# First layer: Q and K of head 0 for both halves of the tokens from a float32 product ahead of the norm

## The chip, the cores and the metric

The kernel runs on one core of a Trainium2 chip. What counts is the time of one execution on the device, in microseconds (us). All inputs and outputs are float32.

## The reference

A decoder of two layers works on 1024 tokens of width 1024. Each layer normalises h, makes one input projection from it, runs two groups of heads side by side and adds their output projection to h; then it adds a gated feed-forward part:

```
u = rmsnorm(h, attn_norm[l])
rq, rk, rv, rg, dq, dk, dv = split(u @ w_in[l])
ret = silu(rg) * rmsnorm(retention_chunkwise(rq, rk, rv))
dif = rmsnorm(diff_attention(dq, dk, dv, lam)) * (1 - lam_init)
h = h + concat(ret, dif) @ w_out[l]
u = rmsnorm(h, ffn_norm[l])
h = h + (silu(u @ w_gate[l]) * (u @ w_up[l])) @ w_down[l]
```

The change touches only the start of the first layer: its rmsnorm, and dq, dk, dv of head 0. Differential attention has four heads. Each head has two softmaxes of 64 channels and uses their difference; it is causal, with a bias that falls with distance. The norm's factor is one number per token, so it may be put on before a projection or after it. The norm's gains are one number per channel and may be folded into the weights.

## The kernel before

Everything is kept channels by tokens: h is eight tiles of 128 channels by 1024 tokens. The tokens are worked in two halves of 512. A product that must be nearly float32 is made in the faster float32r format: each operand is split into a high and a low part, and three matmuls of the parts (high by high, high by low, low by high) go into the same PSUM bank (`mm3`, L288 to L290, for a weight as the stationary operand; `tm_pair`, L323 to L325, for the values, where the tokens are stationary). A weight is split by a cast on ScalarE (L280) and a subtraction on GpSimd (L281); it stands in tiles named `w`, of which there are 12. The normalised tokens are split in `norm_half`: VectorE multiplies (L446), ScalarE casts (L448), VectorE or, for two of the eight tiles of half 0, GpSimd subtracts (L450).

The norm of a half comes in three steps. ScalarE squares and VectorE sums (L426, L433); TensorE adds over the channels with small matmuls (L398); a few tiny operations make the factor of each token, and TensorE spreads it over the partitions by transposing it (L414, into a bank of tag `s`). Then the 24 large operations of the split follow.

K and Q of head 0 for half 0 are special in the first layer. `fm_first` (L307) multiplies h itself, ahead of the norm, by weights into which the gains are folded (L1232), in full float32. When the factor is there, it is put on as the product leaves PSUM (L696), and `stack` writes the high part (L522, ScalarE) and the low part (L523, VectorE) of K and Q into stacked tiles. K and Q of half 1 are made after the norm, with `mm3`.

TensorE runs its instructions in the order in which the program writes them; on the other engines a scheduler chooses the order, and each engine then runs it strictly in a row, as does SyncE's queue of DMAs. The program's order around the change is: K of half 0, Q of half 0, with the norm's small matmuls in between; the values of half 0, with the transposes of half 1's norm (L414) between them; then head 0. Attention goes over eight blocks of 128 queries. `att_block` makes the scores of softmax 1 (L574, L575, into one of two banks of tag `s`), then of softmax 0, then transposes the weights of the block before (`att_turn`, L600). VectorE adds the bias and takes the maximum (L577, L580), ScalarE takes the exponential (L581), VectorE the reciprocal of the sum (L582) and the weighting (L656), ScalarE scales (L657), VectorE combines both (L666), and the transposes of this block need that. Every second block, `att_out` multiplies by the values (L619 to L622) and ScalarE copies the result (L624).

So that TensorE need not wait for that chain, `weave` puts matmuls of something else between the steps. It is given two totals: each unit of the attention draws total of fill by total of attention. The attention of blocks 0 to 3 has 72 units, its fill 96: 48 for K and Q of half 1 and 48 for the values of half 1. Blocks 4 to 7 are filled with K and Q of head 1. If the fill runs out early, the attention's steps stand alone.

Of the kernel before, what the change touches and what calls it, by code (L numbers as in the profile page):

```python
# [13 lines left out]
R32 = mybir.dt.float32r  # L14
AF = mybir.ActivationFunctionType
ALU = mybir.AluOpType
AX = mybir.AxisListType

P = 128
D = 1024  # L20
T = 1024
KT = D // P
NH = 2
HT = T // NH
# [95 lines left out]
class Line:  # L120
# [17 lines left out]
    def run(self, end):  # L138
        self.todo()
        while self.n + 1 < end:  # L140
            self.n += 1
            go, after = self.products[self.n]
            yield from go()
            self.todo()
            after()


class Trunk:
# [152 lines left out]

    def fm_first(self, h, ws):

        for w in ws:
            ps = self.bank("mm")
            for k in range(KT):
                self.nc.tensor.matmul(ps, lhsT=w[:, P * k:P * k + P], rhs=h[k][:, 0:HT], start=k == 0,  # L307
                                      stop=k == KT - 1)
                yield 4
            self.first_ps.append(ps)  # L310

    def tm_pair(self, w2, u, tt):
        ps = self.bank("mm")
# [122 lines left out]
    def norm_half(self, h, hf, gcol, us, lag=11, gap=9, first=False, keep=False):  # L436
        nc = self.nc
        sl = slice(hf * HT, hf * HT + HT)
        parts = self.squares(h, sl, 0, True, first)
        yield lag  # L440
        y = yield from self.rsqrt_rows(parts, D, gap=gap)
        hi = self.t("u", 4, [P, KT, HT], R32)
        lo = self.t("u", 4, [P, KT, HT], R32)
        for k in range(KT):
            f = self.tmp()
            nc.vector.scalar_tensor_tensor(out=f, in0=h[k][:, sl], scalar=self.gains[:, gcol + k:gcol + k + 1],  # L446
                                           in1=y, op0=ALU.mult, op1=ALU.mult)
            nc.scalar.copy(hi[:, k], f)  # L448
            eng = nc.gpsimd if keep and k in (1, 4) else nc.vector
            eng.tensor_tensor(out=lo[:, k], in0=f, in1=hi[:, k].bitcast(F32), op=ALU.subtract)  # L450
        if keep:
            self.first_y = self.big("sp")[:, 0:HT]
            nc.scalar.copy(self.first_y, y)
        us[hf] = (hi, lo)

    def seven_first(self, h, gcol, b, keep):
# [230 lines left out]
    def attention(self, l, us, w_first, norm1):  # L687
        wk, wq, wdv = w_first
        nc = self.nc
        v, qk, outs = {}, self.qk_tiles(), []  # L690
        kq = lambda hf: self.chain(self.stacks(wk, us, (hf,), qk[1], 1.0), self.stacks(wq, us, (hf,), qk[0], 0.125))
        first = [self.chain(kq(hf), self.values(wdv, us, hf, v)) for hf in range(NH)]
        if l == 0:
            for ps, st, scale in zip(self.first_ps, (qk[1], qk[0]), (1.0, 0.125)):
                f = self.tmp()
                nc.vector.tensor_tensor(out=f, in0=ps, in1=self.first_y, op=ALU.mult)  # L696
                self.stack(f, st, slice(0, HT), scale)
            self.weave(norm1, 40, self.values(wdv, us, 0, v), 48)
            self.late_consts()
        else:  # L700
            self.weave(norm1, 96, first[0], 96)
        self.prev, self.norms, self.outs = None, [], []
        for h in range(4):
            o = self.big("mx")
            outs.append(o)
            A = self.att_open(h, qk, v, o)
            nqk = self.qk_tiles() if h < 3 else None
            self.att_swap(A, 0)
            if h:
                self.att_swap(A, 1)  # L710
            if h == 0:
                self.weave(self.att_part(l, A, 0, 4), PART0, first[1], 96)
                self.att_swap(A, 1)
            elif h == 2:
                self.weave(self.att_part(l, A, 0, 4), PART0, self.values(wdv, us, 1, v), 48)
            if h == 3:
                rq = [self.big("ka") for _ in range(2)]
                rk = [self.big("a4") for _ in range(2)]
                fill = self.chain(self.ret_proj(us, rq[0], 1.0), self.ret_proj(us, rq[1], 1.0),
                                  self.ret_proj(us, rk[0], 0.125), self.ret_proj(us, rk[1], 0.125))  # L720
            else:
                fill = self.qk_head(us, nqk)
            if h % 2:
                self.weave(self.att_part(l, A, 0, 8), PART0 + PART1, fill, 96 if h == 1 else 192)
            else:
                self.weave(self.att_part(l, A, 4, 8), PART1, fill, 96)
            if h < 3:
                qk = nqk
            if h == 1:
                wdv = [self.weight(), self.weight()]  # L730
                v = {}
                self.weave(self.att_close(l), 48, self.values(wdv, us, 0, v), 48)
        return outs, rq, rk
# [481 lines left out]
    def run(self):  # L1215
        nc = self.nc
        self.nf = 0
        h = [self.big("a4") for _ in range(KT)]
        raws = [self.big("wr") for _ in range(2)]
        fold = [self.big("sp") for _ in range(2)]  # L1220

        def load(hf, ks):
            sl = slice(hf * HT, hf * HT + HT)
            for k in ks:
                nc.sync.dma_start(h[k][:, sl], self.a["xT"][k][:, sl])

        def load_w(i, c):
            cs = slice(512 * c, 512 * c + 512)
            nc.sync.dma_start(raws[i][:, cs], self.a["wts"][i][:, cs])
            g = self.gains[:, 4 * c:4 * c + 4].rearrange("p (k o) -> p k o", o=1).broadcast_to([P, 4, P])  # L1230
            v = lambda t: t[:, cs].rearrange("p (k m) -> p k m", m=P)
            nc.vector.tensor_tensor(out=v(fold[i]), in0=v(raws[i]), in1=g, op=ALU.mult)  # L1232

        def some(n):
            for _ in range(n):
                next(early)
        us, nus = {}, {}
        for c in range(2):
            load_w(0, c)
            load(0, range(4 * c, 4 * c + 4))  # L1240
        for c in range(2):
            load_w(1, c)
        self.wi = 2
        self.first_ps = []
        early = self.fm_first(h, fold)
        norm0 = self.norm_half(h, 0, 0, us, keep=True, gap=14)
        norm1 = self.norm_half(h, 1, 0, us, 8, 14, True)
        next(norm0)
        some(6)
        next(norm0)  # L1250
        load(1, range(KT))
        next(norm1)
        some(4)
        self.drain(norm0, early)
        wk, wq = [self.weight(raw=r) for r in raws]
        wdv = [self.weight(), self.weight("mx")]
        w_first = (wk, wq, wdv)
        h = self.layer(0, h, us, w_first, norm1, lambda h: [self.norm_half(h, 0, 8, nus)])
        h = self.layer(1, h, nus, self.first_weights(), self.norm_half(h, 1, 8, nus, 34),
                       lambda h: [self.final(h, 0, HT, 0), self.final(h, HT, 256, 0)])  # L1260
        self.drain(self.final(h, HT + 256, 256, 1))
# [28 lines left out]
```

## Time and profile before

| | us |
|---|---|
| median of three runs | 2290.36 (2289.78 to 2291.29) |
| the profiled execution's own time | 2289.39 |
| its span, first to last instruction | 2287.6 |
| TensorE busy | 2251.1 |
| VectorE busy | 1404.7 |
| ScalarE busy | 1009.1 |
| GpSimd busy | 731.7 |

In the profile PE is TensorE's matmuls, PEld its weight loads, DVE VectorE, ACT ScalarE, POOL GpSimd, SP SyncE. A row of the timeline gives the start, the duration, the engine, the source line, the operation, the tile written and the tiles read, and how many instructions are merged; behind it in brackets the idle time before it and who ended it. The end of a matmul is modelled, so the distance of two starts tells more of TensorE's pace than the duration of one. A float32 matmul of 128x512 shows as two records. In the table of windows the number behind the busy times is the clock that TensorE was granted, 1.00 being full. Names such as `ps_mm` are tiles: `ps_` means PSUM.

### The profile page before, as it was taken

How to read it: one execution, taken by the hardware profiler on the slowest of the kernel's cores; microseconds unless marked ns; L12 is line 12 of the kernel's file. 1: busy time of each engine (PE TensorE's matmuls, PEld its weight loads, DVE VectorE, ACT ScalarE, POOL GpSimd, SP SyncE). 2: the span in 40 equal slices, each digit the busy share in tenths (PEclk: the TensorE clock that was granted, in tenths of full speed). 3: DMA queues.
4: the chain of work that ended last, by engine and by line, in shares of the span. 5: the costliest groups of instructions: out<-in, count | busy, mean ns of one | idle time of the engine just before them, and what ended most of it. 6: DMA issues, size and time to landing. Idle time of an engine off the chain costs nothing.

```text
span 2287.6 us, 30632 instructions
## 1 busy us (share of the span) xinstructions
PE 2251.1 (98%) x11328; PEld 1895.3 (83%) x11328; DVE 1404.7 (61%) x2596; ACT 1009.1 (44%) x1905; POOL 731.7 (32%) x588
## 2 busy tenths in 40 slices
PE   7999999999999999999999999999999999999998
PEld 5888898787888888888888888988878888888887
DVE  8777612989534333995567774059884434359856
ACT  5666523445333333543256665234453333344332
POOL 3111212120455555335121112211215445544350
PEclk9999999999999999999999999999999999999999
DMA  4212121112433333652232222112123232346422
GB/s 164 79 47 65 44 95 38 55 57 63 137 106 103 105 106 90 230 186 96 72 99 56 56 65 88 52 37 74 49 95 120 93 115 93 110 148 202 157 65 74
DMA packets 74215, 216.58 MB, mean 95 GB/s; under 512 B 8017, under 2 KB 10065, under 8 KB 74065
## 3 DMA queue, kind: packets, MB, share of 16 engines
q1 hardware_dynamic: 74064, 214.62, 29.1%
q8 instruction: 89, 1.46, 0.3%
q14 instruction: 62, 0.50, 0.1%
HBM read 162.16 MB, written 44.04 MB: 90 GB/s over the span
## 4 chain that ended last, share of the span: by engine, by line
PE 84%; DVE 11%; ACT 2%; issue 1%; DMA 1%; POOL 0%; SPq 0%; DVEq 0%; ACTq 0%; POOLq 0%
PE ps_mm L264 8%; PE ps_mm L265 8%; PE ps_mm L266 8%; PE ps_mm L289 7%; PE ps_mm L288 7%; PE ps_mm L290 7%; PE ps_s L265 4%; PE ps_s L264 4%; PE ps_s L266 4%; PE ps_mm L323 3%; PE ps_mm L324 3%; PE ps_mm L325 3%; PE ps_t L265 2%; PE ps_t L264 2%; PE ps_t L266 2%
## 5 line engine op out<-in xcount | busy, mean ns | idle before, releaser
L241 POOL TENSOR_TENSOR w<-wr,w 128x512 fp32r<-128x512 f32 x262 | 368.2, 1419 | 442.9 <-ACT w L240 425.6
L281 POOL TENSOR_TENSOR w<-wr,w 128x512 fp32r<-128x512 f32 x140 | 186.2, 1337 | 577.3 <-ACT w L280 520.7
L288 PE MATMUL ps_mm<-u,w 128*128 128x512 f32 (+1 forms) x735 | 296.1, 403 | 0.0
L289 PE MATMUL ps_mm<-u,w 128*128 128x512 f32 (+1 forms) x735 | 287.2, 391 | 2.4 <-DVE u L450 2.4
L290 PE MATMUL ps_mm<-u,w 128*128 128x512 f32 (+1 forms) x735 | 286.5, 390 | 0.0
L240 ACT CAST w<-wr 128x512 fp32r<-128x512 f32 x312 | 187.2, 619 | 136.5 <-DVE wr L911 77.5
L264 PE MATMUL ps_mm<-u,w 128*128 128x512 f32 x432 | 168.5, 390 | 0.0
L266 PE MATMUL ps_mm<-u,w 128*128 128x512 f32 x432 | 168.1, 389 | 0.0
L265 PE MATMUL ps_mm<-u,w 128*128 128x512 f32 x432 | 168.1, 389 | 0.0
L290 PEld LDWEIGHTS ps_mm<-u,w 128*128 128x128 f32 x735 | 138.1, 188 | 30.1
L289 PEld LDWEIGHTS ps_mm<-u,w 128*128 128x128 f32 x735 | 138.6, 189 | 26.0 <-DVE u L450 3.1
L288 PEld LDWEIGHTS ps_mm<-u,w 128*128 128x128 f32 x735 | 138.3, 188 | 23.7
L960 ACT COPY t<-ps_mm 128x512 f32<-128x512 f32 x76 | 44.7, 588 | 240.3 <-PE ps_mm L266 240.3
L280 ACT CAST w<-wr 128x512 fp32r<-128x512 f32 x140 | 85.7, 619 | 128.6 <-PE ps_t L289 39.6
L325 PE MATMUL ps_mm<-w,u 128*128 128x256 f32 x448 | 127.2, 284 | 0.8 <-DVE u L450 0.8
L323 PE MATMUL ps_mm<-w,u 128*128 128x256 f32 x448 | 128.0, 286 | 0.0
L324 PE MATMUL ps_mm<-w,u 128*128 128x256 f32 x448 | 126.9, 283 | 0.0
L241 POOL TENSOR_TENSOR w<-t,w 128x512 fp32r<-128x512 f32 x48 | 65.1, 1357 | 191.9 <-ACT w L240 191.9
L577 DVE CUSTOM_DVE_ANT_0 sp<-ps_s,wr 128x512 f32<-128x512 f32 (+2 forms) x192 | 102.9, 552 | 32.3 <-PE ps_s L575 31.3
L581 ACT ACTIVATE sp<-sp,m 128x256 f32<-128x256 f32 (+7 forms) x128 | 99.2, 775 | 50.2 <-DVE m L580 49.4
L869 DVE TENSOR_TENSOR a<-a,ps_mm 128x512 f32<-128x512 f32 (+1 forms) x148 | 98.6, 667 | 27.6 <-PE ps_mm L266 14.5
L909 DVE TENSOR_TENSOR t<-wr,wr 128x512 f32<-128x512 f32 x46 | 32.8, 712 | 119.2 <-DMA wr<-wts 118.5
(386 smaller groups left out, 5919.7 us busy)
## 6 DMA issues: line engine op xcount, KB each, us to landing
wr<-wts SPq DMA_DIRECT2D x190, 512.0 KB, 3.7
mx<-s_fast SPq DMA_DIRECT2D x56, 512.0 KB, 4.9
s_fast<-mx SPq DMA_DIRECT2D x48, 512.0 KB, 4.8
kb<-ka SPq DMA_DIRECT2D x64, 128.0 KB, 2.3
s_rest<-mx SPq DMA_DIRECT2D x12, 512.0 KB, 2.9
kb<-wts SPq DMA_DIRECT2D x12, 512.0 KB, 5.4
mx<-s_rest SPq DMA_DIRECT2D x12, 512.0 KB, 3.3
a<-xT SPq DMA_DIRECT2D x16, 256.0 KB, 5.4
```

Of the source, the lines that this page charges most:

```text
L240: nc.scalar.copy(h, src)
L241: (eng or nc.gpsimd).tensor_tensor(out=o, in0=src, in1=h.bitcast(F32), op=ALU.subtract)
L264: mm(ps, lhsT=wh[:, c], rhs=bh, start=first and i == 0, stop=False, skip_group_check=True)
L265: mm(ps, lhsT=wh[:, c], rhs=bl, start=False, stop=False, skip_group_check=True)
L266: mm(ps, lhsT=wl[:, c], rhs=bh, start=False, stop=i == 3, skip_group_check=True)
L281: nc.gpsimd.tensor_tensor(out=o, in0=raw[:, cols], in1=h.bitcast(F32), op=ALU.subtract)
L288: mm(out, lhsT=lh, rhs=rh, start=first, stop=False)
L289: mm(out, lhsT=lh, rhs=rl, start=False, stop=False)
L290: mm(out, lhsT=ll, rhs=rh, start=False, stop=last)
L323: mm(o, lhsT=uh, rhs=wh, start=k == 0, stop=False)
L324: mm(o, lhsT=uh, rhs=wl, start=False, stop=False)
L325: mm(o, lhsT=ul, rhs=wh, start=False, stop=k == KT - 1)
```

## The change

`fm_first` now makes four products instead of two: K and Q of half 0 into two `mm` banks, K and Q of half 1 into the bank of tag `o` and one of tag `t`, each of eight float32 matmuls. `first_stacks` puts the factors on and writes the stacked tiles, for each half once its norm is done. The stacked tiles of head 0 come from other pools (`mx`, `ka`), since those of `h` are still read. The weights of K and Q are no longer split. Both halves' norms are now given by the same helper, the factor of half 1 is kept too, and the whole of it stands ahead of the values of half 0, which are no longer woven with the norm. Blocks 0 to 3 of head 0 still have a fill total of 96, but only the values of half 1 (48) are left in it.

```diff
     def fm_first(self, h, ws):
-        for w in ws:
-            ps = self.bank("mm")
+        for (hf, w), tag in zip([(hf, w) for hf in range(NH) for w in ws], ("mm", "mm", "o", "t")):
+            ps = self.bank(tag)
+            self.first_ps.append(ps)
             for k in range(KT):
-                self.nc.tensor.matmul(ps, lhsT=w[:, P * k:P * k + P], rhs=h[k][:, 0:HT], start=k == 0,
-                                      stop=k == KT - 1)
+                self.nc.tensor.matmul(ps, lhsT=w[:, P * k:P * k + P], rhs=h[k][:, HT * hf:HT * hf + HT],
+                                      start=k == 0, stop=k == KT - 1)
                 yield 4
-            self.first_ps.append(ps)
+
+    def first_stacks(self, qk, hf):
+        for ps, st, scale in zip(self.first_ps[2 * hf:], (qk[1], qk[0]), (1.0, 0.125)):
+            f = self.tmp()
+            self.nc.vector.tensor_tensor(out=f, in0=ps, in1=self.first_y[hf], op=ALU.mult)
+            self.stack(f, st, slice(HT * hf, HT * hf + HT), scale)
...
-            eng = nc.gpsimd if keep and k in (1, 4) else nc.vector
+            eng = nc.gpsimd if keep and hf == 0 and k in (1, 4) else nc.vector
...
-        first = [self.chain(kq(hf), self.values(wdv, us, hf, v)) for hf in range(NH)]
+        first = [self.chain(*([] if l == 0 else [kq(hf)]), self.values(wdv, us, hf, v)) for hf in range(NH)]
         if l == 0:
-            for ps, st, scale in zip(self.first_ps, (qk[1], qk[0]), (1.0, 0.125)):
-                f = self.tmp()
-                nc.vector.tensor_tensor(out=f, in0=ps, in1=self.first_y, op=ALU.mult)
-                self.stack(f, st, slice(0, HT), scale)
-            self.weave(norm1, 40, self.values(wdv, us, 0, v), 48)
+            self.drain(first[0])
...
-        norm0 = self.norm_half(h, 0, 0, us, keep=True, gap=14)
-        norm1 = self.norm_half(h, 1, 0, us, 8, 14, True)
+        self.first_y = []
+        self.first_qk = [self.big("mx", R32) for _ in range(2)], [self.big("ka", R32) for _ in range(2)]
+        norm0, norm1 = [self.norm_half(h, hf, 0, us, first=True, keep=True) for hf in range(NH)]
         next(norm0)
-        some(6)
+        some(8)
         next(norm0)
         load(1, range(KT))
         next(norm1)
-        some(4)
-        self.drain(norm0, early)
-        wk, wq = [self.weight(raw=r) for r in raws]
-        wdv = [self.weight(), self.weight("mx")]
-        w_first = (wk, wq, wdv)
-        h = self.layer(0, h, us, w_first, norm1, lambda h: [self.norm_half(h, 0, 8, nus)])
+        some(3)
+        self.drain(norm0)
+        some(5)
+        self.first_stacks(self.first_qk, 0)
+        some(8)
+        next(norm1)
+        some(3)
+        self.drain(norm1, early)
+        self.first_stacks(self.first_qk, 1)
+        w_first = (None, None, [self.weight(), self.weight()])
+        h = self.layer(0, h, us, w_first, None, lambda h: [self.norm_half(h, 0, 8, nus)])
```

The lines of the changed kernel differ: L308 is the float32 matmul (before L307), L404 and L420 the norm's small matmuls and transposes (L398, L414), L329 to L331 the values (L323 to L325), L452, L454 and L456 the split (L446, L448, L450), L315 the product with the factor (L696), L528 and L529 `stack` (L522, L523), L580 and L581 the scores (L574, L575), L606 the transposes (L600), L587 the exponential (L581), L663 the scaling (L657), L630 the copy of the output (L624); L280 and L288 to L290 keep theirs.

TensorE's queue at the end of the start-up, before the change (`ps_mm_193` is Q of half 0, `ps_s_294` the sums of half 1's norm, `ps_mm_308` the values of half 0):

```order
L307 MATMUL ps_mm_193<-a_19_94,sp_100 128x512
L307 MATMUL ps_mm_193<-a_20_95,sp_100 128x512
L307 MATMUL ps_mm_193<-a_21_96,sp_100 128x512
L398 MATMUL ps_s_294<-c_ones,acc_168 128x1 x4
L323 MATMUL ps_mm_308<-w_261,u_201 128x256
L324 MATMUL ps_mm_308<-w_262,u_201 128x256
L325 MATMUL ps_mm_308<-w_261,u_202 128x256
```

The same place now (`ps_o_259` and `ps_t_281` are K and Q of half 1, `ny_275` is the factor of half 1's norm):

```order
L308 MATMUL ps_o_259<-a_21_96,sp_99 128x512
L404 MATMUL ps_s_269<-c_ones,acc_174 128x1 x4
L308 MATMUL ps_t_281<-a_14_89,sp_100 128x512
L308 MATMUL ps_t_281<-a_15_90,sp_100 128x512
L308 MATMUL ps_t_281<-a_16_91,sp_100 128x512
L420 MATMUL ps_s_285<-c_ident,ny_275 128x128 x4
L308 MATMUL ps_t_281<-a_17_92,sp_100 128x512
L308 MATMUL ps_t_281<-a_18_93,sp_100 128x512
L308 MATMUL ps_t_281<-a_19_94,sp_100 128x512
L308 MATMUL ps_t_281<-a_20_95,sp_100 128x512
L308 MATMUL ps_t_281<-a_21_96,sp_100 128x512
L329 MATMUL ps_mm_365<-w_345,u_206 128x256
```

Before, the values of half 0 stood ahead of the transposes of half 1's norm; now they stand behind them and behind five float32 matmuls.

TensorE's queue at the transposes of block 2, before (`ps_mm_674` is the fill, values of half 1; `ps_t_733` the transposes):

```order
L323 MATMUL ps_mm_674<-w_265,u_350 128x256
L324 MATMUL ps_mm_674<-w_266,u_350 128x256
L325 MATMUL ps_mm_674<-w_265,u_351 128x256
L600 MATMUL ps_t_733<-c_ident,sp_594 128x128 x3
L323 MATMUL ps_mm_674<-mx_271,u_350 128x256
L324 MATMUL ps_mm_674<-mx_272,u_350 128x256
L325 MATMUL ps_mm_674<-mx_271,u_351 128x256
```

The changed kernel from its last matmul of fill on (`ps_s_652`, `ps_s_662` are the scores of block 2, `ps_t_669` the transposes of block 1, `ps_s_678`, `ps_s_696` the scores of block 3, `ps_t_707` the transposes of block 2):

```order
L331 MATMUL ps_mm_568<-w_359,u_291 128x256
L580 MATMUL ps_s_652<-ka_120,mx_118 128x384
L581 MATMUL ps_s_652<-kb_484,mx_118 128x384
L580 MATMUL ps_s_662<-ka_119,mx_117 128x384
L581 MATMUL ps_s_662<-kb_483,mx_117 128x384
L606 MATMUL ps_t_669<-c_ident,sp_588 128x128 x2
L580 MATMUL ps_s_678<-ka_120,mx_118 128x512
L581 MATMUL ps_s_678<-kb_484,mx_118 128x512
L625 MATMUL ps_o_685<-a_124_632,v_363 128x256
L626 MATMUL ps_o_685<-a_124_632,v_364 128x256
L625 MATMUL ps_o_685<-a_124_632,v_363 128x256
L626 MATMUL ps_o_685<-a_124_632,v_364 128x256
```

Blocks 2 and 3 now have no fill between their steps; it comes back with `ps_mm_743` (K of head 1) behind the first scores of block 4.

ScalarE's queue at block 2 in the changed kernel (`m_651`, `m_661` are maxima of block 2, `w_1100` the high part of a weight of head 1, `wr_1098` the raw weight as loaded):

```order
L587 ACTIVATE sp_649,z_650<-sp_649,m_651 128x384
L630 COPY mx_482<-ps_o_685 128x256
L280 CAST w_1100<-wr_1098 128x512
L587 ACTIVATE sp_649,z_650<-sp_649,m_661 128x384
L663 ACTIVATE sp_649<-sp_649,z_650 128x384
L587 ACTIVATE sp_675,z_676<-sp_675,m_677 128x512
```

A cast that needs a weight from memory stands there between the two exponentials of block 2; before, the rows between them were these:

```order
L581 ACTIVATE sp_594,z_595<-sp_594,m_596 128x384
L657 ACTIVATE sp_594<-sp_594,z_595 128x384
L581 ACTIVATE sp_594,z_595<-sp_594,m_624 128x384
L605 CAST a_123_569<-ps_t_644 128x2x128
L546 CAST v_585<-ps_mm_587 128x512
```

Behind block 4 of head 0 every engine has the same instructions in the same order as before, but for the names of tiles.

More of the change, by code (lines that the diff above doesn't have):

```diff
@@ L448, in norm_half @@
             nc.scalar.copy(hi[:, k], f)
-            eng = nc.gpsimd if keep and k in (1, 4) else nc.vector
+            eng = nc.gpsimd if keep and hf == 0 and k in (1, 4) else nc.vector
             eng.tensor_tensor(out=lo[:, k], in0=f, in1=hi[:, k].bitcast(F32), op=ALU.subtract)
         if keep:
-            self.first_y = self.big("sp")[:, 0:HT]
-            nc.scalar.copy(self.first_y, y)
+            self.first_y.append(self.big("sp")[:, 0:HT])
+            nc.scalar.copy(self.first_y[hf], y)
         us[hf] = (hi, lo)
@@ L689, in attention @@
         nc = self.nc
-        v, qk, outs = {}, self.qk_tiles(), []
+        v, qk, outs = {}, self.first_qk if l == 0 else self.qk_tiles(), []
         kq = lambda hf: self.chain(self.stacks(wk, us, (hf,), qk[1], 1.0), self.stacks(wq, us, (hf,), qk[0], 0.125))
-        first = [self.chain(kq(hf), self.values(wdv, us, hf, v)) for hf in range(NH)]
+        first = [self.chain(*([] if l == 0 else [kq(hf)]), self.values(wdv, us, hf, v)) for hf in range(NH)]
         if l == 0:
-            for ps, st, scale in zip(self.first_ps, (qk[1], qk[0]), (1.0, 0.125)):
-                f = self.tmp()
-                nc.vector.tensor_tensor(out=f, in0=ps, in1=self.first_y, op=ALU.mult)
-                self.stack(f, st, slice(0, HT), scale)
-            self.weave(norm1, 40, self.values(wdv, us, 0, v), 48)
+            self.drain(first[0])
             self.late_consts()
```

## The prediction

> **What bounds the kernel now.** I read the page first: span, busy shares and the chain of work that ended last.
>
> ```profile
> span 2287.6 us, 30632 instructions
> PE 2251.1 (98%) x11328; PEld 1895.3 (83%) x11328; DVE 1404.7 (61%) x2596; ACT 1009.1 (44%) x1905; POOL 731.7 (32%) x588
> PE 84%; DVE 11%; ACT 2%; issue 1%; DMA 1%; POOL 0%; SPq 0%; DVEq 0%; ACTq 0%; POOLq 0%
> ```
>
> TensorE is the bound, so what TensorE loses or wins at the start is lost or won for the whole. Then I read the timeline of TensorE up to block 4 of head 0.
>
> ```profile
> 14.07 1.05 PE L398 MATMUL ps_s<-c_ones,acc 128*128 128x1 f32 x8 [1.22 <-DVE acc L433]
> 14.98 5.38 PE L307 MATMUL ps_mm<-a,sp 128*128 128x512 f32 x8
> 20.20 0.60 PE L414 MATMUL ps_s<-c_ident,ny 128*128 128x128 f32 x4
> 20.63 5.32 PE L307 MATMUL ps_mm<-a,sp 128*128 128x512 f32 x12
> 27.55 1.02 PE L398 MATMUL ps_s<-c_ones,acc 128*128 128x1 f32 x8 [1.60 <-DVE acc L433]
> 28.43 0.36 PE L323 MATMUL ps_mm<-w,u 128*128 128x256 f32 x1
> ...
> 38.34 0.62 PE L414 MATMUL ps_s<-c_ident,ny 128*128 128x128 f32 x4 [0.66 <-DVE ny L410]
> ...
> 45.99 0.40 PE L288 MATMUL ps_mm<-u,w 128*128 128x512 f32 x1
> 46.22 0.40 PE L289 MATMUL ps_mm<-u,w 128*128 128x512 f32 x1
> ...
> 59.23 0.28 PE L323 MATMUL ps_mm<-w,u 128*128 128x256 f32 x1
> 59.34 0.28 PE L324 MATMUL ps_mm<-w,u 128*128 128x256 f32 x1
> ...
> 73.54 0.40 PE L574 MATMUL ps_s<-ka,a 128*128 128x512 f32 x1
> 74.24 0.40 PE L288 MATMUL ps_mm<-u,w 128*128 128x512 f32 x1
> ```
>
> The values of half 0 run from 28.43 to 45.99, K and Q of half 1 with blocks 0 and 1 to 59.23, the values of half 1 with blocks 2 and 3 to 73.54. At 74.24 the fill for blocks 4 to 7 begins; from there on the change alters nothing but names. So the question is when the changed kernel gets to that instruction. Prices from the starts: 0.23 us for a split matmul 512 wide, 0.12 for one 256 wide, and 0.44 for a float32 record (5.32 over 12), so 0.87 for a float32 matmul. All this at full clock, which the table of windows qualifies:
>
> ```profile
> 12.94:16.35 3.41, 2.28 (x11) 1.57 (x12) 3.31 (x4) 1.70 (x4) 2.68 (x2) 1.00 1.05 387
> 16.35:19.77 3.42, 3.42 (x6) 1.35 (x5) 2.74 (x7) 2.03 (x5) 0.94 (x2) 0.50 1.05 407
> 26.59:30.00 3.41, 2.44 (x19) 2.27 (x19) 3.41 (x5) 2.33 (x5) 3.41 (x3) 1.00 0.20 24
> 30.00:36.83 6.83, 4.63 (x20) 4.34 (x21) 6.80 (x11) 4.00 (x7) 3.15 (x3) 0.50 0.42 143
> 36.83:40.25 3.42, 2.76 (x24) 2.59 (x24) 2.48 (x7) 0.88 (x3) 0.00 (x0) 1.00 0.73 156
> ```
>
> After 3.4 us with about 1 us of idling and 1 us of the tiny sums L398, the clock is halved for 3.4 us (16.35) or 6.8 us (30.00).
>
> **Removed.** K and Q of half 1: 48 x 0.23 = 11.0 us of TensorE, all on the path. The splitting of two raw weights, off the path.
>
> **Added.** 16 float32 matmuls, 16 x 0.87 = 13.9 us: dearer than what they replace, so the change wins only where they fill waiting. Eleven stand ahead of half 1's transposes, five (4.3 us) behind. Putting on the factor and stacking half 1 costs VectorE little more than before (two products).
>
> **Half 1's transposes.** VectorE sets them:
>
> ```profile
> 9.26 0.69 DVE L1232 TENSOR_TENSOR sp<-wr,c_gains 128x512 f32<-128x512 f32 x1
> 13.93 3.44 DVE L1232 TENSOR_TENSOR sp<-wr,c_gains 128x512 f32<-128x512 f32 x2
> 13.67 3.15 POOL L281 TENSOR_TENSOR w<-wr,w 128x512 fp32r<-128x512 f32 x2 [2.59 <-ACT w L280]
> 20.83 0.75 DVE L446 SCALAR_TENSOR_TENSOR t<-a,c_gains,ps_s 128x512 f32<-128x512 f32 x1
> 34.83 1.28 DVE L696 TENSOR_TENSOR t<-ps_mm,sp 128x512 f32<-128x512 f32 x2
> 36.20 1.40 DVE L523 SCALAR_TENSOR_TENSOR ka<-t,ka 64x512 fp32r<-64x512 f32 x2
> 39.00 2.06 DVE L446 SCALAR_TENSOR_TENSOR t<-a,c_gains,ps_s 128x512 f32<-128x512 f32 x3 [0.81 <-PE ps_s L414]
> 50.22 1.97 DVE L450 TENSOR_TENSOR u<-t,u 128x512 fp32r<-128x512 f32 x2
> ```
>
> Without GpSimd's splitting beside them, the two folds take 2 x 0.69 instead of 3.44. TensorE does the first product whole from 12.85 on (14.07 less its idling; four more records, 1.7), then the sums (1.05), then six records (2.6), so half 0's transposes come near 18.2 if the clock holds and 20.7 if it halves as before. VectorE has four sums of half 1 (0.7 each, like a fold) queued ahead, so I let the split start at 19.4, 1.4 sooner than 20.83. One sum fewer stands inside it, so it ends at 34.83 - 2.1 = 32.7. Then come two products (1.3), four low parts ahead of the factor instead of two (2.8), and the small operations (0.9: before, 37.60 to 38.34, and one read): the transposes at 37.7, against 38.34; 39.8 if nothing is gained at the start. Behind that wait TensorE's queue holds all values of half 0, which before stood ahead of it.
>
> **Values of half 0.** TensorE is through its eleven early float32 matmuls by 33.6 (from 18.8: sixteen matmuls, 13.9, and the sums, 1.05) and waits 4 us for the transposes, so the clock will be half after them. Five float32 matmuls take 4.3 at full and 8.7 at half clock; I take 6.1, since the windows end at 40.25 or 43.66. Then 96 matmuls x 0.12 = 11.5: 37.7 + 0.6 + 6.1 + 11.5 = **55.9**, between 54.1 and 60.4. Before it was 45.99: 9.9 later, and the splitting of half 1 (done by 52.2 even before) is no longer in the way. Two other moves have cover. VectorE's stacking of half 1 now waits behind its read of the first values, to about 53, but block 4 is the first to need it. On SyncE the bias of head 1 now stands ahead of the copies of K for block 0; they are free to go near 38 and needed near 60, which covers them five times (a load takes 3.7, row below); without that cover each microsecond would count.
>
> **Blocks 0 and 1 with the fill.** Fill goes at 96 to 72, as before, but there are 48 units: the head's 12 units, block 0 (12) and most of block 1 use it up. 11.5 + eight scores (1.0) + a transpose (0.1) = 12.6: to **68.5**.
>
> **Blocks 2 and 3 bare.** TensorE's own work there to the next fill is 3.6 (four scores 384 wide at 0.18, eight others 512 or 256 wide, six matmuls of the output, five transposes). But transposes wait for the softmax chain:
>
> ```profile
> 59.94 0.34 PE L574 MATMUL ps_s<-ka,a 128*128 128x384 f32 x1
> 60.12 0.34 PE L575 MATMUL ps_s<-kb,a 128*128 128x384 f32 x1
> 61.11 0.56 DVE L577 CUSTOM_DVE_ANT_0 sp<-ps_s,wr 128x384 f32<-128x384 f32 x1
> 61.90 0.62 ACT L581 ACTIVATE sp<-sp,m 128x384 f32<-128x384 f32 x1 [0.19 <-DVE m L580]
> 63.09 0.62 ACT L657 ACTIVATE sp<-sp,z 128x384 f32<-128x384 f32 x1 [0.48 <-DVE z L656]
> 64.76 0.62 DVE L666 SCALAR_TENSOR_TENSOR sp<-sp,z 128x384 f32<-128x384 f32 x1
> 65.29 0.42 DVE L606 TENSOR_TENSOR a<-ps_t,a 128x256 fp32r<-128x256 f32 x1
> 67.14 0.69 DVE L547 TENSOR_TENSOR v<-ps_mm,v 128x512 fp32r<-128x512 f32 x1
> 71.78 0.49 PE L600 MATMUL ps_t<-c_ident,sp 128*128 128x128 f32 x3
> L280 ACT CAST w<-wr 128x512 fp32r<-128x512 f32 x140 | 85.7, 619 | 128.6 <-PE ps_t L289 39.6
> wr<-wts SPq DMA_DIRECT2D x190, 512.0 KB, 3.7
> ```
>
> Before, block 2's first scores stood 11.8 us ahead of its transposes, and the chain took 61.11 to 65.38 (64.76 + 0.62), 4.3 us of it. Bare, from the last fill: block 1's combining ends near 0.9 (its own exponential stands behind the cast of a weight whose tile the fill frees last), the read of block 2's first scores at 1.4, and that of its second, queued behind two low parts (0.69 and 0.42), at 3.3. The second exponential stands behind the cast of a weight (`w_1100`), whose load can start only when an earlier weight is split (about 0.5) and takes 3.7: cast (0.62) 4.2 to 4.8, exponential with its sum to 5.8, scaling (0.62) to 6.4, combining to 7.1, transposes to 7.5, scores of block 4 to **8.2**. The bounds are 3.6 (TensorE's own work) and 10 (two chains of 4.3 and the cast's wait, nothing overlapped); I take the steps, since the queues fix their order.
>
> **The clock there.** In those 8.2 us TensorE idles some 4.6. By the row 26.59 that halves the clock; the next 3.4 us then do half their work, a loss of 1.7 (3.4 for two windows). Sum: 68.5 + 8.2 + 1.7 = 78.4 against 74.24, **4.2 us later**. By the Trainium skill's page "TensorE: Matmul & The Clock Gate", Part 1, the clock falls only after a whole window (about 3.4 us) of idling; by that rule this term would be nothing, and it is a rival below. That page's window length agrees with the rows here; its condition does not, since 2.44 us of busy time stood in the window 26.59.
>
> **Rivals.**
> 1. *The chain keeps up.* If the softmaxes of blocks 2 and 3 hide, the bare stretch is TensorE's 3.6 and the clock holds: 55.9 + 12.6 + 3.6 = 72.1, 2.1 sooner: 2288.3. For it: VectorE and ScalarE have no other work there. Against it: 4.3 us of chain and one weight load per step.
> 2. *The half clock stays (slower).* The wait of 4 us ahead of half 1's transposes covers more than a window, and row 30.00 shows two slow windows in a row. If the transposes come at 39.8 and the clock stays low for 6.8 us after them, the values of half 0 start late and slowly: 39.8 + 0.6 + 8 + 11.5 = 59.9, 4.0 beyond my 55.9, so 8.2 in all: 2298.6. It decides from a wait of one window (3.4) on; it needs the late start too.
> 3. *The clock holds in the bare stretch.* Its idling is cut into pieces by scores and transposes. Then 1.7 falls away: +2.5, 2292.9. For it: row 36.83, where 0.66 of idling did not halve it. Against it: the last gap alone is over 3 us.
>
> **How the numbers follow.** The profiled execution took 2289.39 (span 2287.6), 1.0 less than the median 2290.36; I put the difference on the median: 2290.36 + 4.2 = 2294.6. A measurement can tell about 0.2%, 4.6 us, so my forecast stands just inside "no change". Chances: the forecast 0.46, with a range of its own from +1.5 to +6.5, of which 0.26 lies within 4.6 and 0.20 above; rival 1 0.14 (0.02 of it faster by over 4.6: the values at 54.1 and no bare wait give 3.9, so it needs a little more); rival 2 0.22, all slower; rival 3 0.13 (0.12 within); something unnamed 0.05 (faster 0.03, within 0.01, slower 0.01). That makes faster 0.05, same 0.51, slower 0.44. The range leaves out most of rival 1 and the end of rival 2: -0.9 to +8.0, 2289.5 to 2298.4.
>
> **What would show it.** In the changed profile: half 1's transposes (L420) near 37.7, a granted clock of 0.50 behind them, the first scores of block 0 near 60, no matmul of fill from about 68.5 until K of head 1 (L288) near 78, and waits for L672 ahead of L606 of block 2. I am wrong if L288 of head 1 stands before 74 (then the chain was hidden) or if TensorE waits somewhere behind block 4 for longer than before.

## The result and the profile after

The changed kernel takes 2296.68 us (median of 10 runs), the kernel before 2290.05 us in 10 runs beside it. The ratio is 1.0028 with a 95% interval of 1.0018 to 1.0038: slower by 6.6 us, by 4.1 to 8.7. Single runs of this and of three other kernels took far longer (2510 us here, at a granted clock of 0.84 instead of 0.996), and the ratios leave them out. The profiled execution took 2295.36 us, with a span 6.0 us longer than before.

The page of the changed kernel: its head, the busy time of the engines, and the chain of work that ended last.

```profile
span 2293.6 us, 30590 instructions
PE 2254.8 (98%) x11312; PEld 1892.1 (82%) x11312; DVE 1405.2 (61%) x2598; ACT 1008.0 (44%) x1902; POOL 723.9 (32%) x584
PE 85%; DVE 10%; ACT 2%; issue 2%; DMA 1%; POOL 0%; DVEq 0%; SPq 0%; ACTq 0%; POOLq 0%
```

TensorE's busy time is 3.7 us more, the chain's shares are nearly those of before, and nothing on this page tells where 6 us went. They are lost on TensorE by the second scores of block 4, at 83 us. Its timeline in the changed kernel (start, duration, engine, line, tiles, count; in brackets the idle time ahead and who ended it):

```profile
31.00 2.82 PE L308 MATMUL ps_t<-a,sp 128*128 128x512 f32 x6
40.12 1.09 PE L420 MATMUL ps_s<-c_ident,ny 128*128 128x128 f32 x4 [6.30 <-DVE ny L416]
41.00 6.46 PE L308 MATMUL ps_t<-a,sp 128*128 128x512 f32 x10
46.90 0.68 PE L329 MATMUL ps_mm<-w,u 128*128 128x256 f32 x1
47.42 0.28 PE L330 MATMUL ps_mm<-w,u 128*128 128x256 f32 x1
...
63.13 0.28 PE L580 MATMUL ps_s<-ka,mx 128*128 128x256 f32 x1
...
71.40 0.34 PE L580 MATMUL ps_s<-ka,mx 128*128 128x384 f32 x1
...
72.59 0.44 PE L606 MATMUL ps_t<-c_ident,sp 128*128 128x128 f32 x2 [0.33 <-DVE sp L672]
...
78.39 0.52 PE L606 MATMUL ps_t<-c_ident,sp 128*128 128x128 f32 x3 [3.12 <-DVE sp L672]
...
79.67 0.63 PE L288 MATMUL ps_mm<-u,w 128*128 128x512 f32 x1
80.10 0.63 PE L289 MATMUL ps_mm<-u,w 128*128 128x512 f32 x1
```

Two waits carry the loss. TensorE stands for 6.30 us ahead of the transposes of half 1's norm (L420), which come at 40.12 where before they came at 38.34 after a wait of 0.66. And between 71.40 and 79.67, with no product left to fill it, it stands for 3.12 us ahead of the transposes of block 2. K of head 1 (L288) begins at 79.67 instead of 74.24, 5.4 late, and its first products start 0.43 us apart instead of 0.23: the clock is halved. With that the transposes of block 7 come 6.8 late (118.30 against 111.47). Behind that the kernel waits no longer in all than before (16 us against 17); on the whole it gives 0.8 us back, so that 6.0 are left.

Why L420 came so late is seen on VectorE and GpSimd, in the same columns. VectorE in the changed kernel:

```profile
19.50 0.74 DVE L452 SCALAR_TENSOR_TENSOR t<-a,c_gains,ps_s 128x512 f32<-128x512 f32 x1
...
28.91 2.05 DVE L452 SCALAR_TENSOR_TENSOR t<-a,c_gains,ps_s 128x512 f32<-128x512 f32 x3
30.88 4.37 DVE L456 TENSOR_TENSOR u<-t,u 128x512 fp32r<-128x512 f32 x3
35.17 1.27 DVE L315 TENSOR_TENSOR t<-ps_mm,sp 128x512 f32<-128x512 f32 x2
...
36.55 1.40 DVE L529 SCALAR_TENSOR_TENSOR ka<-t,ka 64x512 fp32r<-64x512 f32 x2
37.98 1.41 DVE L529 SCALAR_TENSOR_TENSOR mx<-t,mx 64x512 fp32r<-64x512 f32 x2
```

GpSimd in the changed kernel:

```profile
30.08 1.27 POOL L456 TENSOR_TENSOR u<-t,u 128x512 fp32r<-128x512 f32 x1
31.31 3.39 POOL L281 TENSOR_TENSOR w<-wr,w 128x512 fp32r<-128x512 f32 x2
```

The last three subtractions of the split (L456) took 4.37 us. The same three in VectorE's timeline of the kernel before:

```profile
32.68 2.22 DVE L450 TENSOR_TENSOR u<-t,u 128x512 fp32r<-128x512 f32 x3
```

Beside them GpSimd splits two tiles of a weight (L281, 3.39 us). That weight is the first one of head 1, needed at 79.67. By the code, the split weights of K and Q of head 0 are no longer made and one weight of the values has moved into the tiles `w`; four tiles are free, and the next weight in line is split into them here. In the kernel before GpSimd's first split behind 32 us comes at 49.75.

### The profile page after: what moved, and what is told of

It reads as the page before. It is cut to its first block, busy times and chain, and to the rows that moved or that the text cites. A ratio compares the mean times of both kernels' runs of the same rounds, so it can differ in the third digit from the quotient of the medians.

```text
span 2293.6 us, 30590 instructions
## 1 busy us (share of the span) xinstructions
PE 2254.8 (98%) x11312; PEld 1892.1 (82%) x11312; DVE 1405.2 (61%) x2598; ACT 1008.0 (44%) x1902; POOL 723.9 (32%) x584
## 4 chain that ended last, share of the span: by engine, by line
PE 85%; DVE 10%; ACT 2%; issue 2%; DMA 1%; POOL 0%; DVEq 0%; SPq 0%; ACTq 0%; POOLq 0%
PE ps_mm L264 8%; PE ps_mm L265 8%; PE ps_mm L266 8%; PE ps_mm L288 7%; PE ps_mm L289 7%; PE ps_mm L290 6%; PE ps_s L264 4%; PE ps_s L265 4%; PE ps_s L266 4%; PE ps_t L264 3%; PE ps_t L266 3%; PE ps_t L265 3%; PE ps_mm L329 2%; PE ps_mm L330 2%; PE ps_mm L331 2%
## 5 line engine op out<-in xcount | busy, mean ns | idle before, releaser
L281 POOL TENSOR_TENSOR w<-wr,w 128x512 fp32r<-128x512 f32 x138 | 184.0, 1340 | 586.0 <-ACT w L280 528.7
L288 PE MATMUL ps_mm<-u,w 128*128 128x512 f32 x719 | 290.3, 404 | 0.0
L289 PE MATMUL ps_mm<-u,w 128*128 128x512 f32 x719 | 281.3, 391 | 1.2 <-DVE u L456 1.2
L290 PE MATMUL ps_mm<-u,w 128*128 128x512 f32 x719 | 280.7, 390 | 0.0
L264 PE MATMUL ps_mm<-u,w 128*128 128x512 f32 x432 | 168.6, 390 | 0.0
L266 PE MATMUL ps_mm<-u,w 128*128 128x512 f32 x432 | 168.1, 389 | 0.0
L265 PE MATMUL ps_mm<-u,w 128*128 128x512 f32 x432 | 168.1, 389 | 0.0
L290 PEld LDWEIGHTS ps_mm<-u,w 128*128 128x128 f32 x719 | 135.3, 188 | 29.7
L289 PEld LDWEIGHTS ps_mm<-u,w 128*128 128x128 f32 x719 | 136.0, 189 | 24.0 <-DVE u L456 1.7
L288 PEld LDWEIGHTS ps_mm<-u,w 128*128 128x128 f32 x719 | 135.7, 189 | 23.4
L280 ACT CAST w<-wr 128x512 fp32r<-128x512 f32 x138 | 84.6, 620 | 122.7 <-PE ps_t L289 39.6
L329 PE MATMUL ps_mm<-w,u 128*128 128x256 f32 x480 | 137.2, 286 | 0.0
L331 PE MATMUL ps_mm<-w,u 128*128 128x256 f32 x480 | 135.7, 283 | 0.0
L330 PE MATMUL ps_mm<-w,u 128*128 128x256 f32 x480 | 135.7, 283 | 0.0
L587 ACT ACTIVATE sp<-sp,m 128x256 f32<-128x256 f32 (+7 forms) x128 | 99.1, 774 | 55.9 <-DVE m L586 55.3
```

The costliest lines, as they stand in the source:

```text
L264: mm(ps, lhsT=wh[:, c], rhs=bh, start=first and i == 0, stop=False, skip_group_check=True)
L265: mm(ps, lhsT=wh[:, c], rhs=bl, start=False, stop=False, skip_group_check=True)
L266: mm(ps, lhsT=wl[:, c], rhs=bh, start=False, stop=i == 3, skip_group_check=True)
L281: nc.gpsimd.tensor_tensor(out=o, in0=raw[:, cols], in1=h.bitcast(F32), op=ALU.subtract)
L288: mm(out, lhsT=lh, rhs=rh, start=first, stop=False)
L289: mm(out, lhsT=lh, rhs=rl, start=False, stop=False)
```

## The experiments

Each kernel is timed beside the kernel before on its own chip, and set against the changed kernel by way of that: "-5.9 against the changed kernel" is its difference to before less the 6.6 us above. Each ratio is known to about 2 us, so a difference between two experiments of under 3 us rests on their traces, not on their times. The traces themselves stand apart by up to 1.4 us at the start already (the transposes of half 0 come between 17.63 and 19.05), so a moment in one kernel against the same in another is good to about that; waits and distances inside one trace are not touched by it.

**The bare stretch.** The fill of blocks 0 to 3 in the first layer (half 1's values, 48 units) is paced for 96, so it is used up by block 1. One number paces it for 48:

```
-                self.weave(self.att_part(l, A, 0, 4), PART0, first[1], 96)
+                self.weave(self.att_part(l, A, 0, 4), PART0, first[1], 96 if l else 48)
```

> The changed kernel with one number altered: the fill total of blocks 0 to 3 of head 0 in the first layer is 48 instead of 96, so the values of half 1 are spread over all four blocks. Theory A (the bare softmax chain of blocks 2 and 3 costs some 4.7 us beyond TensorE's own work, and the halved clock behind it 1.6): the time falls by 4.5 to 6.4 us against the changed kernel, no wait of over 1 us ahead of the transposes of block 2, clock 1.00 behind block 3. Theory B (the loss is the dearer float32 products and the late start of the values, the chain would be late anyway): it falls by less than 1.5 us.

Measured: 2290.6 us (ratio 1.0006, 0.9997 to 1.0015), 0.7 above before, so -5.9 against the changed kernel. The waits of TensorE in its first part (18 to 130 us; the columns are the total, how often, the longest):

```profile
PE ps_s L420 <- DVE ny L416: 5.4, 1, 5.4
PE ps_t L606 <- DVE sp L672: 0.9, 1, 0.9
```

The long wait ahead of half 1's transposes stays (5.4 instead of 6.3, since half 0's split ended 1.05 sooner in this execution). The 3.5 us ahead of the transposes of blocks 1 and 2 are gone: the 0.9 of the second line stand at 128.53, in head 1, and the kernel before has 0.7 at that place. The granted clock is 1.00 from 64 to 84, and K of head 1 begins at 74.34. The bare stretch with its clock is worth most of the loss, as theory A had it.

**The late values.** Half 0's values are brought back ahead of half 1's transposes: three of their sixteen parts (18 products) and all of the float32 product stand ahead of the transposes, the rest behind them:

```
         next(norm1)
-        some(3)
-        self.drain(norm1, early)
+        self.drain(early)
+        wdv, self.first_v = [self.weight(), self.weight()], {}
+        fill = self.values(wdv, us, 0, self.first_v)
+        for _ in range(3):
+            next(fill)
+        self.drain(norm1)
         self.first_stacks(self.first_qk, 1)
...
```

> The changed kernel with TensorE's queue altered at the start: all sixteen float32 matmuls of K and Q of half 1, its eight of Q whole, and three steps of the values of half 0 stand ahead of half 1's transposes, the rest of the values behind. Theory A (TensorE's 6.3 us of waiting and the half clock behind it are lost because the values stand behind the transposes): the wait falls under 1 us, the clock stays at 1.00, the values of half 0 end near 51 instead of 58.8, and the time falls by 6 to 8.5 us; the bare stretch of blocks 2 and 3 stays. Theory B (VectorE's split of half 1 sets the start, whatever TensorE does before): it falls by less than 2 us.

Measured: 2289.51 us (0.9993, 0.9984 to 1.0002), -7.0 against the changed kernel. TensorE no longer waits ahead of L420 (at 39.14), blocks begin at 53.24 instead of 63.13, and the bare stretch is still there, with waits of 0.7 and 3.3 us:

```profile
69.07 0.52 PE L606 MATMUL ps_t<-c_ident,sp 128*128 128x128 f32 x3 [3.31 <-DVE sp L672]
```

But in the profiled execution the clock held behind it, and the products of head 1 started 0.23 us apart. This kernel's times lie in two groups (2286 to 2287.4 and 2289.4 to 2290.9); that the clock falls in some executions and not in others would give that. The mean granted clocks fit it (0.998 to 0.999 in the four of the first group, 0.997 in five of the six of the second, 0.998 in the sixth); a trace of the second group was not taken.

**The collision.** GpSimd's early split of head 1's first weight is put behind the last cast of half 1's split, some 20 us later; nothing else is edited:

```
-            nc.scalar.copy(hi[:, k], f)
+            self.last_cast = nc.scalar.copy(hi[:, k], f)
...
     def qk_head(self, us, qk, behind=None):
-        yield from self.stacks(self.weight(), us, (0, 1), qk[1], 1.0)
+        with self.tc.issue_after(behind.ins) if behind else nullcontext():
+            w = self.weight()
+        yield from self.stacks(w, us, (0, 1), qk[1], 1.0)
...
-            fill = self.qk_head(us, nqk)
+            fill = self.qk_head(us, nqk, self.last_cast if l == 0 and h == 0 else None)
```

> The changed kernel with the cast of the first weight of head 1 queued on ScalarE behind the last cast of half 1's split, so that GpSimd's two subtractions for it no longer run beside VectorE's split of half 0. Theory A (they cost VectorE 2.3 us there and so made half 1's transposes late: 40.1 instead of the 37.7 predicted): VectorE's last three subtractions of half 0 take 2.0 instead of 4.4 us, the transposes come near 37.8, and the time falls by 1 to 3 us. Theory B (the transposes are late for another reason, the four low parts queued ahead of the factor): within 0.7 us of the changed kernel.

Measured: 2293.41 us (1.0016, 1.0007 to 1.0025), -3.1 against the changed kernel. VectorE in this kernel:

```profile
30.68 2.22 DVE L456 TENSOR_TENSOR u<-t,u 128x512 fp32r<-128x512 f32 x3
32.82 1.28 DVE L315 TENSOR_TENSOR t<-ps_mm,sp 128x512 f32<-128x512 f32 x2
```

and TensorE's waits in its first part, where lines behind 540 are two further down than in the changed kernel:

```profile
PE ps_s L420 <- DVE ny L416: 4.2, 1, 4.2
PE ps_t L608 <- DVE sp L674: 3.6, 2, 3.2
```

The three subtractions are back at 2.22, the split ends at 32.82 (35.17), the transposes come at 37.77 (40.12), and all behind them moves up by 2.3: K of head 1 begins at 77.36. Of these 2.3 us 0.2 are an earlier start of this trace and 2.15 the collision; the two waits, 4.2 and 3.6, stay. The collision itself has only moved: GpSimd now splits at 51.35 and 54.48, and half 1's low parts (L529) beside it take 4.5 us instead of 2.8. Here TensorE doesn't wait for them.

**The clock.** Ten products of 128x512 in the fast format, whose result nobody reads, are put into the 3.12 us ahead of the transposes of block 2 in the changed kernel. They compute nothing that is used:

```
         if prev:
             B, k, q = prev
+            if l == 0 and A["h"] == 0 and i == 3:
+                ps = self.bank("mm")
+                for _ in range(10):
+                    nc.tensor.matmul(ps, lhsT=A["q"][0][:, 0:P], rhs=A["k"][0][:, 0:512], start=True, stop=True)
             self.att_turn(B, k, q)
```

> The changed kernel with ten more products of 128x512 in the fast format into a bank that nobody reads, placed between the scores of block 3 and the transposes of block 2, where TensorE waited 3.12 us. They compute nothing that is used. Theory A (the half clock behind the bare stretch is the price of TensorE's idle time in it): the first products behind the stretch start 0.23 us apart instead of 0.43, the first of them still at about 79.7 on the trace's scale, and the time falls by 1 to 1.8 us below the changed kernel's 2296.7 (6.6 above before becomes about 5). Rival B (those products start 0.43 apart for another reason, such as their weights arriving late): still 0.43 apart, the time is the same or up to 1 us longer.

Measured: 2294.56 us (1.0017, 1.0008 to 1.0026), 4.2 above before, so -2.4 against the changed kernel with more work. Windows of 2 us, first of the changed kernel (after the length: busy time of PE, PEld, DVE, ACT and POOL with counts, then the granted clock, the DMA share and GB/s):

```profile
74.00:76.00 2.00, 1.23 (x7) 0.59 (x5) 2.00 (x11) 1.11 (x4) 0.00 (x0) 1.00 0.47 178
76.00:78.00 2.00, 0.00 (x0) 0.00 (x0) 0.59 (x3) 2.00 (x5) 1.26 (x1) 1.00 0.00 0
78.00:80.00 2.00, 1.61 (x8) 1.52 (x9) 1.24 (x5) 2.00 (x7) 0.00 (x0) 0.79 0.00 0
80.00:82.00 2.00, 2.00 (x6) 1.52 (x6) 1.68 (x7) 0.81 (x3) 1.37 (x1) 0.50 0.00 0
```

and of the kernel with the ten products:

```profile
74.00:76.00 2.00, 1.97 (x12) 1.59 (x11) 2.00 (x11) 0.97 (x3) 0.00 (x0) 1.00 0.53 217
76.00:78.00 2.00, 1.82 (x9) 1.17 (x7) 0.60 (x5) 1.87 (x5) 1.17 (x1) 1.00 0.00 0
78.00:80.00 2.00, 1.32 (x9) 1.23 (x10) 1.32 (x5) 2.00 (x6) 0.11 (x1) 1.00 0.00 0
80.00:82.00 2.00, 2.00 (x10) 1.66 (x9) 1.89 (x7) 0.88 (x3) 1.08 (x1) 1.00 0.00 0
```

K of head 1 begins at the same moment (79.73 against 79.67), but its products start 0.23 us apart, ten records in 80 to 82 instead of six. The second scores of block 4 come at 81.80 instead of 83.10, 1.3 sooner; that much of the 2.4 us the trace explains, and the rest is within what a ratio can tell. The clock held in more than this one execution: its mean is 0.997 in ten of the eleven runs, against 0.996 in all nine of the changed kernel that stand in its ratio. So the half clock is the price of TensorE's idle time in the bare stretch, and nothing else is late there: weights and scores were ready.

**The two together, then three and four.** The first two edits were run together.

> The two edits together: fill total 48 and the values of half 0 partly ahead of half 1's transposes. Theory A (two separate losses that add): 9 to 14 us faster than the changed kernel, so 3 to 7 us faster than the kernel before; block 4's fill starts near 68 to 70. Theory B (one loss that both edits cure, or a new wait for the split of half 1 that eats it): no more than 8 us faster than the changed kernel, about level with before.

Measured: 2286.98 us (0.9986, 0.9977 to 0.9995), -9.5 against the changed kernel. That is inside theory A's 9 to 14, though less than the two gains of 5.9 and 7.0 together; each alone gives back about all of the loss, which fits a change that is a gain without its losses. K of head 1 begins at 70.68. A new wait stands ahead of block 0's second scores, for VectorE's first biases and maxima, and the clock is half for 3.4 us behind it (58.7 to 62.1). TensorE and then VectorE in this kernel:

```profile
57.61 0.39 PE L580 MATMUL ps_s<-ka,mx 128*128 128x256 f32 x1 [2.46 <-DVE m L583]
```

```profile
53.34 0.68 DVE L553 TENSOR_TENSOR v<-ps_mm,v 128x512 fp32r<-128x512 f32 x1
54.05 1.40 DVE L529 SCALAR_TENSOR_TENSOR ka<-t,ka 64x512 fp32r<-64x512 f32 x2
55.49 1.40 DVE L529 SCALAR_TENSOR_TENSOR mx<-t,mx 64x512 fp32r<-64x512 f32 x2
56.92 0.43 DVE L215 TENSOR_TENSOR t<-t 128x256 f32<-128x256 f32 x1
57.26 0.28 DVE L583 CUSTOM_DVE_ANT_0 sp<-ps_s,wr 128x128 f32<-128x128 f32 x1
```

The four low parts of half 1's K and Q (L529, 2.8 us), which no block below 4 reads, have priority over the softmax of block 0. Two more kernels take that up from both sides. The first adds the edit on the collision to the two:

> All three single edits together: half 1's values spread over blocks 0 to 3, half 0's values brought ahead of half 1's transposes, and GpSimd's split of head 1's first weight put behind half 1's split. Theory A (the three places are three separate terms, and the third one only counts where TensorE waits for half 1's transposes, which it no longer does once half 0's values stand ahead of them; but VectorE also reaches block 0's softmax the 2 us earlier): first scores' wait for VectorE shrinks from 2.46 us to 0.5 to 1.5, the time is 1 to 2.5 us below that of the two edits alone (2286.98), 2284.5 to 2286. Rival B (the collision does nothing once the wait ahead of the transposes is gone): within 0.7 us of 2287.0, and the 2.46 us wait stays.

Measured: 2288.99 us (0.9992, 0.9983 to 1.0002), 1.3 below before, where the two alone were 2.9 below. Both theories miss. The wait is longer (3.42 instead of 2.46), because the split of head 1's weight, sent away from one stretch of VectorE, landed in the next; and the clock is half there for 6.8 us instead of 3.4 (56.3 to 63.1). VectorE and GpSimd in this kernel:

```profile
52.84 2.36 DVE L529 SCALAR_TENSOR_TENSOR ka<-t,ka 64x512 fp32r<-64x512 f32 x2
55.23 1.41 DVE L529 SCALAR_TENSOR_TENSOR mx<-t,mx 64x512 fp32r<-64x512 f32 x2
```

```profile
51.37 2.56 POOL L281 TENSOR_TENSOR w<-wr,w 128x512 fp32r<-128x512 f32 x2 [5.38 <-ACT w L280]
```

The pair beside GpSimd takes 2.36, the pair behind it 1.41. The second kernel leaves the collision where it was in the two edits and puts the stacking of half 1 behind block 1, without priority:

```
-            self.stack(f, st, slice(HT * hf, HT * hf + HT), scale)
+            if hf:
+                self.late.append((f, st, slice(HT, 2 * HT), scale))
+            else:
+                self.stack(f, st, slice(0, HT), scale)
...
-    def stack(self, ps, st, sl, scale):
+    def stack(self, ps, st, sl, scale, hurry=True):
...
-            with self.tc.high_priority():
+            with self.tc.high_priority() if hurry else nullcontext():
...
             yield from self.att_block(l, A, i, self.prev)
+            if i == 1:
+                while self.late:
+                    self.stack(*self.late.pop(0), hurry=False)
```

> The two edits (values of half 1 spread, values of half 0 brought forward) and a third: the stacking of half 1's K and Q (four copies on ScalarE, four subtractions on VectorE), needed from block 4 on, is put behind block 1's softmax instead of ahead of everything. Theory A (VectorE's queue ahead of block 0's first bias step is what is late): the 2.46 us wait ahead of block 0's second scores goes to under 0.6 us, the half clock behind it goes with it, and the time falls by 2 to 4 us below 2287.0, to 2283 to 2285. Rival B (block 0's softmax is late for its own chain, not for those subtractions): the wait stays above 1.5 us and the time is within 1 us of 2287.0.

Measured: 2286.35 us (0.9982, 0.9974 to 0.9991), 4.0 below before and 1.1 further than the two edits. TensorE's waits in the first part of this kernel, whose lines behind 530 stand three further down than with the two edits:

```profile
PE ps_t L609 <- DVE sp L675: 3.0, 2, 2.3
```

Theory A holds at its place, but not in the time: the 2.46 us wait for the maxima is gone and the clock stays full, and K of head 1 begins at 68.24, 2.4 sooner (0.6 of it an earlier start of the trace). But 2.3 us of waiting stand now ahead of the transposes of block 0, for its softmax, and of the 2.4 us the profiled span keeps 0.5. Some 1.6 of the rest is in two waits between 900 and 1200 us, for casts of a weight, which the kernel with two edits doesn't have; why they came was not tried. All four edits together:

> All four edits together. Theory A (they remove the waits of the three places that the changed kernel shows, and the new one): no wait over 1 us at TensorE between the split of half 1 and block 4; 2282 to 2284.5, which is 12 to 15 us below the changed kernel and 5.5 to 8 us below the kernel before. Rival B (the removed waits come back elsewhere, for example at block 4's transposes or in a half clock of the sustained product): 2286 or more.

Measured: 2285.82 us (0.9980, 0.9971 to 0.9989): 4.5 below before, 11.1 below the changed kernel, the lowest of all, and short of the 5.5 to 8 that were expected, if not so far as the rival had it. Its trace shows the rival's mechanism: ahead of block 0's transposes there is a wait of 2.4 us, and the clock is half for 3.4 us from 59.2 on (TensorE's row, then the window of 60 to 62 us in the columns of above):

```profile
59.64 0.48 PE L611 MATMUL ps_t<-c_ident,sp 128*128 128x128 f32 x1 [2.42 <-DVE sp L677]
60.00:62.00 2.00, 2.00 (x10) 2.00 (x10) 1.81 (x4) 0.42 (x2) 0.00 (x0) 0.50 0.16 33
```

The last two kernels can't be told apart by their times.

## Why the prediction came out as it did

The forecast was 2294.6 and slower by 4.2; measured were 2296.68 and 6.6, inside the range, but beyond the bound of 4.6 which the forecast had put itself just within: "no change", to which it gave 0.51, didn't come. The way in which the time is lost was right but for one step. Step by step:

- **The start.** Half 0's split at 19.4: measured 19.50. That the folds are quick without GpSimd's splits is right.
- **Half 1's transposes at 37.7.** This step failed: 40.12. The sum took the split's end from the row of before, less the earlier start (1.4) and one sum (0.7), 34.83 - 2.1 = 32.7, and thereby let its last subtractions stay at 2.22 us. It did not ask what GpSimd would now do. The removed splitting was called "off the path", but the four tiles that it no longer holds pull the next weight's split forward, into VectorE's subtractions: +2.15 there, and the split ended at 35.17. With that split out of the way, the transposes came at 37.77: the rest of the step is right. The prediction's bound of 39.8, "if nothing is gained at the start", was passed for another reason than it named.
- **The wait of 4 us and five float32 matmuls at 6.1.** Measured 6.30; and 41.00 to 46.90: 5.9. With the collision taken out the wait was 4.15.
- **Values of half 0 end at 55.9.** 58.8: the 2.4 of the transposes and 0.5 more, the stretch being 18.7 us long instead of 18.2: 0.3 in the transposes themselves, at half clock, and 0.4 ahead of the second product of the values (46.90, 47.42), less 0.2 in the float32 matmuls.
- **Blocks 0 and 1 with the fill, 12.6.** 58.8 to 71.40: 12.6.
- **Blocks 2 and 3 bare, 8.2.** 71.40 to 79.67: 8.3. The order of its steps held as well; ScalarE in the changed kernel shows the cast that waits for its load between the exponentials of block 2, and the transposes follow 7.0 behind the last fill (forecast 7.5):

```profile
75.86 0.62 ACT L280 CAST w<-wr 128x512 fp32r<-128x512 f32 x1 [0.85 <-DMA wr<-wts]
76.38 0.61 ACT L587 ACTIVATE sp<-sp,m 128x384 f32<-128x384 f32 x1
```

- **The half clock behind it, 1.7.** The products are 0.43 apart from 79.67 to 82.24, 0.23 from then on. Six took 2.6 us instead of 1.4, and the scores ahead of them ran slowly too: from the transposes of block 2 to the second scores of block 4 it was 4.7 us, and 3.1 when the ten products held the clock. The term is real, and at 1.6 nearly of its size; 0.2 of it lie within the 8.3 above and 1.4 behind. By the Trainium skill's page "TensorE: Matmul & The Clock Gate", Part 1, the clock falls only after a whole window of about 3.4 us of idling. The trace agrees with the length (the slow stretch is 3.4 us long), not with that condition: the longest idle ahead of the fall was 3.12 us here, and 2.46 with the two edits. The same section says that the window runs free of the kernel, so that the moment varies; that fits 3.3 us of idling with no fall in the kernel with the early values.
- **Behind block 4 nothing changes.** Right: no wait there is longer by more than 0.2 us (the longest ahead of L606 is 0.9 instead of 0.7), and 0.8 us came back.

The sum: 4.2 forecast, + 2.4 for the transposes, + 0.5 up to the end of the values, + 0.1 in the bare stretch, - 0.3 for the clock (1.4 instead of 1.7, the rest being in the bare stretch) makes 6.9; measured 6.8 at block 7. The time came out at 6.6 because 0.8 us came back behind it and the two medians lie 0.6 further apart than the profiled spans.

The rivals: the chain did not keep up (the first), and the clock did not hold (the third). The second had the late transposes (40.12 against its 39.8) and a half clock of 6.8 us (38.20 to 45.03), but 1.9 us of it fell into the wait, and its price didn't come: the five matmuls and the values behind them took what the forecast had. Its lateness had a cause that no rival named.

And the change itself? Windows of 10 us from 10 to 40, in the columns of above, of the kernel before:

```profile
10.00:20.00 10.00, 8.78 (x23) 4.01 (x22) 8.64 (x12) 5.83 (x13) 4.69 (x4) 0.83 1.05 397
20.00:30.00 10.00, 8.39 (x36) 4.80 (x34) 9.86 (x13) 7.24 (x13) 6.43 (x4) 1.00 0.29 96
30.00:40.00 10.00, 7.15 (x40) 6.68 (x41) 9.03 (x17) 4.63 (x10) 3.15 (x3) 0.66 0.54 151
```

and of the kernel with all four edits:

```profile
10.00:20.00 10.00, 10.00 (x32) 5.07 (x31) 8.08 (x17) 6.49 (x12) 0.52 (x1) 1.00 1.04 393
20.00:30.00 10.00, 10.00 (x25) 4.49 (x24) 10.00 (x15) 7.22 (x13) 7.30 (x5) 1.00 0.34 116
30.00:40.00 10.00, 10.00 (x40) 5.71 (x39) 8.06 (x14) 4.37 (x9) 2.41 (x2) 1.00 0.50 136
```

Before, TensorE was busy for 24.3 of these 30 us, and in parts of them at half clock. The float32 products, with the first values behind them from 38.01, can fill all 30 at full clock. The change as made loses that again: it puts half 0's values behind half 1's transposes, which opens a wait of 6.3 us, and leaves a fill too short for four blocks. With both mended and two queues put in order, the same products make the kernel 4.5 us faster than before (ratio 0.9980, 0.9971 to 0.9989) instead of 6.6 slower. Whether the kernel before would gain from such edits without the products was not tried.

## What to carry to other kernels

When a change takes work away from a pool of buffers, ask what the next in line does with the free ones: which engine starts earlier, and which operation of another engine it will then stand beside. When it shortens the work that fills another chain's waits, pace what is left over the whole chain, and look for the clock behind any gap that opens. And an operation with priority that nobody needs soon is a wait for all that stand behind it: here 2.8 us of low parts ahead of a softmax.

## What the runs showed of the hardware

VectorE's operations with two operands in SBUF and GpSimd's gained next to nothing here by running beside each other. Three subtractions of 128x512 alone take 1.89 us (in the kernel with the two edits, row below) and two of GpSimd's 2.6 (its split at 51.37 with three edits); beside each other VectorE needed 4.37 and GpSimd 3.39, together from 30.88 to 35.25, nearly the sum of 4.5. The multiplications L452, with one operand in PSUM, kept their 0.7 us each beside GpSimd (2.05 for three, 28.91 in the changed kernel).

```profile
43.02 1.89 DVE L456 TENSOR_TENSOR u<-t,u 128x512 fp32r<-128x512 f32 x3
```

The Trainium skill's page "SBUF — State Buffer", section "SBUF: two separate sides", states it so: one port pair is held by one of the two engines for a whole instruction, against VectorE's operations with two SBUF inputs. The rows here agree in the main; that one engine stands still while the other works isn't seen in them.

Two kernels with nearly the same idle time at the same place (2.3 us with the late stacking, 2.4 with all four edits) differ in the clock behind it: full in the one, half for 3.4 us in the other. With the early values it held behind an idle time of 3.3 us, in the changed kernel it fell behind one of 3.1. A gap of 2.3 to 3.3 us may or may not cost the clock here. The row of the late stacking, to be set against the one of all four edits above:

```profile
60.00:62.00 2.00, 2.00 (x19) 2.00 (x17) 1.96 (x6) 0.00 (x0) 0.00 (x0) 1.00 0.00 0
```
